# A two-layer hybrid encoder trunk on one core: expert places read into registers at the first load that needs them, another first buffer, and operands at other offsets

## The chip, the cores and the metric

The kernel runs on one core of one Trainium2 chip. The metric is the device time of one execution in microseconds, and less is better. The kernel before takes 1262.37 us, the median of three runs (1261.83 to 1262.54).

## What is computed

The reference is a trunk of two layers over 256 tokens of width 1024, in float32. Cut to what matters here:

```python
# layer 0
h = h + even_mixer(rmsnorm(h, g0), ...)   # retention heads and a causal convolution of 31 taps
h = h + swiglu(rmsnorm(h, g1), w_gate, w_up, w_down)      # inner width 2816
# layer 1
h = h + odd_mixer(rmsnorm(h, g2), ...)    # gMLP gating and a short convolution of 3 taps
h = h + moe_swiglu(rmsnorm(h, g3), router, e_gate, e_up, e_down)
                                          # 8 experts of inner width 3584, the best 2 for each token
return rmsnorm(h, final_norm)
```

All weights of all eight experts are read in any case: 3 x 1024 x 3584 x 4 bytes for each, 352 MB together, out of some 424 MB that the kernel moves.

## The kernel before

**Dense stages.** The products of layer 0 and of the mixer of layer 1 are made in three parts: each weight unit (1 MB, [128, 2048] float32) is split into a high part `hi` (ScalarE, L169) and a low part `lo` (VectorE, L172), the activations likewise, and `three_products` (L199, L202) sums high x high, low x high and high x low on TensorE. The activations are the weight-loaded operand, and `hi` or `lo` is streamed. Input projections take `xh` and `xl` (class `Norm`) in groups of 12 matmuls over four blocks of 128 rows. The products over rows take `sh`, `sl` (the convolved half of the output projection of layer 0, four blocks), `fh`, `fl` (`rows_product`, the down projection of 22 blocks) and `oyh`, `oyl` (`out_group`, the output projection of layer 1, eight blocks), in groups of six over two blocks, for two halves of the tokens and two of the columns.

**Offsets.** A tile pool gives each tile a fixed place in each partition of SBUF. By the program's allocation `raw`, `hi` and `lo` begin 32 bytes past a multiple of 512, `xh` and `xl` 288 past; in the pools "even" and "ffn" nearly every large tile, `sh`, `sl`, `fh` and `fl` among them, begins 96 past; in the pool "late" the tiles taken after `opc` (`swT`, `y0` with `oyh`, `y1` with `oyl`, `x1`, `x2`) begin 448 past.

**Experts.** The experts are handled in an order of places: place 0 is always expert 0, the others are the experts 1 to 7 by their number of tokens, most first. Which expert stands at a place is known only after routing: `places()` (L1128 on) counts the tokens on TensorE and VectorE, and ends in `idx_i` (L1153), an integer for each place. Each place has room for 96 or 64 tokens (`CAPS`) and is worked in the order `ORDER`, in two parts of 2048 and 1536 hidden columns. A part is 8 gate units and 8 up units (1 MB, or 768 KB in the second part), then 8 or 6 down units of 1 MB of the part before. TensorE works on units straight from the buffer into which they were loaded (`project_step` L1285, `down_step` L1303).

**The loads.** All weights stand in one list, `units`, and all loads are issued on SP's queue, in the order of that list (`Weights._load`, L135). An expert's unit has a callable as its source (`of_expert`), which is called when the load is emitted: for place 0 the address is fixed, for other places it takes `regs[place]`. Expert unit number i goes to `homes[i % 19]`: seven buffers `raw`, then `x1` (`raw_x1`, which held the padded input `spad` of the short convolution), `xl`, four times `hi` and `lo`, `y0` and `y1`. The first 17 are emitted while the output projection of layer 1 still runs, and afterwards `unit` emits, before the products of unit i, the loads up to i + 18. A load waits on SP until its buffer is free, and whatever SP was given after it waits too.

**Where the registers come from.** `places` runs behind unit 1 (the list `later`), and in it seven calls of `values_load` (L1155) read `idx_i` into registers of SP, one after another:

```python
for place in range(1, NE):
    regs[place] = nc.values_load(idx_i[0:1, place:place + 1], engines=(mybir.EngineType.SP,),
                                 min_val=0, max_val=NE - 1)
```

In SP's order they come after load 19 (emitted ahead of unit 1) and before load 20 (emitted ahead of unit 2). The first load that uses a register is number 40, the first gate unit of the second place, emitted ahead of unit 22.

Of the kernel before, what the change touches and what calls it, by code (L numbers as in the profile page):

```python
# [9 lines left out]
F32 = mybir.dt.float32  # L10
# [3 lines left out]
AF = mybir.ActivationFunctionType  # L14
# [4 lines left out]
P = 128  # L19
T = 256  # L20
TB = 2
D = 1024
# [5 lines left out]
CB = CH // P  # L28
# [4 lines left out]
NE = 8  # L33
# [3 lines left out]
N_RAW = 7  # L37
# [61 lines left out]
PE_TAPS = 9  # L99
TAP_CUTS = (6, 4, 16, 13, 13, 11, 10)  # L100
SCR = {"even": 7, "ffn": 5, "late": 6}


def f32(ap):
# [101 lines left out]
def overflow(nc, pool, wpool, small, w_gate, w_up, w_down, e, rank, wgt, slot, hn, h, ident,  # L206
# [5 lines left out]
    nc.vector.tensor_copy(wg, wgt[:, :, ds(e, 1)])  # L212
    oh = pool.tile([P, TB, P], F32, name="oh2", tag="scr", bufs=SCR["late"])
    for tb in range(TB):
# [61 lines left out]
def trunk_kernel(  # L276
# [9 lines left out]
    nc = tc.nc  # L286
# [44 lines left out]
    regs = {}  # L331

    def of_expert(w, place, view):

        def src():
            return view(w[0] if place == 0 else w[ds(regs[place], 1)].rearrange("o k n -> (o k) n"))
        return src

# [22 lines left out]
    wpool = ctx.enter_context(tc.tile_pool(name="weights", bufs=1))  # L361
# [6 lines left out]
    def ps_t():  # L368
        return psum.tile([P, CW], F32, name="pt", tag="pt", bufs=2)
# [5 lines left out]
    h = consts.tile([P, TB, D], F32, name="h")  # L375
# [15 lines left out]
    def load_gain(g, to):  # L391
        nc.sync.dma_start(to, g[0].rearrange("(k p) -> k p", p=P))
# [31 lines left out]
    def scr(pool, name):  # L424
        return pool.tile([P, CW], F32, name=name, tag="scr", bufs=SCR[pool.name])

# [16 lines left out]
    class Norm:  # L443
# [22 lines left out]
                low()  # L466

        def stats(self, tb):
            sq_ = self.pool.tile([P, D], F32, name="sqscr", tag="hid1" if self.pool.name == "late" else "big")
            nc.scalar.activation(sq_, h[:, tb, :], AF.Square, accum_out=self.ss[:, tb:tb + 1])  # L470

        def finish(self):
            rsqrt(self.rstd, self.ss, 1.0 / D)
# [51 lines left out]
    with tc.tile_pool(name="even", bufs=1) as pool, tc.manual_schedule():  # L525
        W.load_to(LOAD_A)
        for i, g in enumerate((e_norm_ffn, o_norm_mix, o_norm_ffn)):
            load_gain(g, gains[1][i * KB:(i + 1) * KB, :])
        prm = pool.tile([P, 2, P], F32, name="prm")
        nc.sync.dma_start(prm[:TAPS * CB, 0, :], e_dw_w[0].rearrange("j (b c) -> (j b) c", c=P))  # L530
        for i, v in enumerate((e_dw_b, e_cv_ln_g, e_cv_ln_b, e_ret_gn)):
            nc.sync.dma_start(prm[i * CB:(i + 1) * CB, 1, :], v[0].rearrange("(b c) -> b c", c=P))
# [75 lines left out]
        pc = pool.tile([P, 2, P], F32, name="pc")  # L608
# [260 lines left out]
    with tc.tile_pool(name="late", bufs=1) as pool:  # L869
# [6 lines left out]
        prm = scr(pool, "oprm")[:, :P]  # L876
# [17 lines left out]
        nc.sync.dma_start(lnb, row(o_sg_ln_b[0], CH))  # L894
        sgw = blocks(scr(pool, "sgw"))
        nc.sync.dma_start(sgw, o_sg_w[0].rearrange("g p q -> p g q"))
        pc = pool.tile([P, CB * 4], F32, name="opc")
        t = ps_t()
        nc.tensor.transpose(t[:, :CB * 4], prm[:CB * 4, :], ident[:CB * 4, :CB * 4])
        nc.vector.tensor_copy(pc, t[:, :CB * 4])  # L900
# [8 lines left out]
        x1 = pool.tile([P, 2 * D], F32, name="spad", tag="x1")  # L909
# [105 lines left out]
        def rt(name, n=NE):  # L1015
            return small.tile([P, TB, n], F32, name=name)
# [10 lines left out]
        with tc.manual_schedule():  # L1027
# [12 lines left out]
            for u in range(KB // 2 - 2):  # L1040
                w = W.next()
                for tb in range(TB):
                    for half in range(2):
# [5 lines left out]
            n = KB * max(CAPS)  # L1049
            rooms = {"xe": [r2[:, i * n:(i + 1) * n].rearrange("p (k n) -> p k n", k=KB) for i in range(2)],  # L1050
                     "oh": r2[:, 2 * n:2 * n + TB * P].rearrange("p (t n) -> p t n", t=TB)}

            homes = ([lambda: wpool.tile([P, 2 * D], F32, name="raw", tag="raw", bufs=N_RAW)] * N_RAW +
                     [lambda: pool.tile([P, 2 * D], F32, name="raw_x1", tag="x1")] +
                     [lambda: consts.tile([P, 2 * D], F32, name="raw_xl", tag="xl")] +
                     [lambda tag=tag: wpool.tile([P, 2 * D], F32, name="raw_" + tag, tag=tag, bufs=4)
                      for _ in range(4) for tag in ("hi", "lo")] +
# [63 lines left out]
        def by_place(dst, src, sel):  # L1121

            for tb in range(src.shape[1]):
                t = pool.tile([P, NE, NE], F32, name="picks", tag="picks", bufs=2)
                nc.vector.tensor_tensor(t, sel, src[:, tb:tb + 1, :].to_broadcast([P, NE, NE]), OP.mult)
                nc.vector.tensor_reduce(dst[:, tb, :], t, axis=AX.X, op=OP.add)

        def places():  # L1128

            pn = ps_t()  # L1130
            nc.tensor.matmul(pn[:, :NE], tri[:, 1, :], both[:, 0, :], start=True, stop=False)
            nc.tensor.matmul(pn[:, :NE], tri[:, 1, :], both[:, 1, :], start=False, stop=True)
            cnt = pool.tile([P, 1, NE], F32, name="cnt")
            nc.vector.tensor_copy(cnt[:, 0, :], pn[:, :NE])
            key = pool.tile([P, NE], F32, name="key")
            nc.vector.tensor_copy(key, cnt[:, 0, :])
            nc.vector.tensor_scalar(key[:, 0:1], key[:, 0:1], 2.0 * T, None, op0=OP.add)
            less = pool.tile([P, NE, NE], F32, name="less")
            nc.vector.tensor_tensor(less, key[:, None, :].to_broadcast([P, NE, NE]),
                                    key[:, :, None].to_broadcast([P, NE, NE]), OP.subtract)  # L1140
            nc.vector.tensor_tensor(less, less, thr[:, 0], OP.is_ge)
            at = pool.tile([P, 1, NE], F32, name="at")
            nc.vector.tensor_reduce(at[:, 0, :], less, axis=AX.X, op=OP.add)
            one = pool.tile([P, 1, NE], F32, name="one")
            nc.vector.tensor_scalar(one, at, 1.0, None, op0=OP.add)
            sel = pool.tile([P, NE, NE], F32, name="sel")
            nc.vector.tensor_tensor(sel, one.to_broadcast([P, NE, NE]),
                                    slot[:, :NE, None].to_broadcast([P, NE, NE]), OP.is_equal)
            idx = pool.tile([P, 1, NE], F32, name="idx")
            by_place(idx, slot[:, None, :NE], sel)  # L1150
            nc.vector.tensor_scalar(idx, idx, -1.0, None, op0=OP.add)
            idx_i = pool.tile([P, NE], I32, name="idx_i")
            nc.vector.tensor_copy(idx_i, idx[:, 0, :])  # L1153
            for place in range(1, NE):
                regs[place] = nc.values_load(idx_i[0:1, place:place + 1], engines=(mybir.EngineType.SP,),  # L1155
                                             min_val=0, max_val=NE - 1)
            ranks = rt("ranks")
            by_place(ranks, rank, sel)

            capacity = pool.tile([P, 1, NE], F32, name="capacity")  # L1160
            nc.vector.tensor_scalar(capacity, at, float(CAPS.index(64, 1)), None, op0=OP.is_ge)
            nc.vector.tensor_scalar(one, at, 0.0, None, op0=OP.is_equal)
            nc.vector.tensor_tensor(capacity, capacity, one, OP.add)
            nc.vector.tensor_scalar(capacity, capacity, -float(96 - 64), 96.0, op0=OP.mult, op1=OP.add)
            nc.vector.tensor_tensor(cnt, cnt, capacity, OP.subtract)
            most = pool.tile([P, 1], F32, name="most")
            nc.vector.tensor_reduce(most, cnt[:, 0, :], axis=AX.X, op=OP.max)
            nc.vector.tensor_scalar(most, most, 0.0, None, op0=OP.max)
            most_i = pool.tile([P, 1], I32, name="most_i")
            nc.vector.tensor_copy(most_i, most)  # L1170
            beyond = rt("beyond")
            for tb in range(TB):
                nc.vector.tensor_tensor(beyond[:, tb, :], rank[:, tb, :], capacity[:, 0, :], OP.subtract)
            gate_of.update(sel=sel, ranks=ranks, beyond=beyond, most_i=most_i)
# [25 lines left out]
        with tc.manual_schedule():  # L1200
# [31 lines left out]
            def results(place, acc, half):  # L1232

                yh = pool.tile([P, CW], F32R, name="eyh", tag="scr", bufs=SCR["late"])
                yl = pool.tile([P, CW], F32R, name="eyl", tag="scr", bufs=SCR["late"])
                n = CAPS[place]
# [115 lines left out]
            todo_[0]()  # L1352
            todo_[1]()
            later += [todo_[2], places, gates]
            acc = was = None
            for i, (place, p) in enumerate(steps):
# [126 lines left out]
```

## Time and profile before

| | |
|---|---|
| runs | 1262.54, 1262.37, 1261.83 us; median 1262.37 |
| the profiled execution | 1261.62 us, its span 1259.7 us |
| granted TensorE clock | 0.995 |
| busy in the span | PE 1213.3 us (96%), PEld 727.1, DVE 355.6, ACT 267.6 |
| DMA | 425.45 MB, mean 338 GB/s |

The span runs from the first to the last instruction; the profiled execution's own time is 1.9 us longer. PE is TensorE's matmuls, PEld its weight loads, DVE VectorE, ACT ScalarE; SPq is the sequencer of SyncE, which issues the DMAs. PE's busy time counts matmuls as they are pipelined, so a high share does not by itself make it the bound. A matmul's own duration overlaps the next one's; how fast matmuls follow each other is read from the times at which they start. The share of DMA is the mean busy share of 16 DMA engines.

### The profile page before, as it was taken

To read this page: it belongs to the slowest core of one execution; us is meant where nothing else is said; L and a number is where in the kernel's file an instruction comes from. 1 tells how busy PE (TensorE), PEld (TensorE's weight loads), DVE (VectorE), ACT (ScalarE), POOL (GpSimd) and SP (SyncE) were. 2 spreads that over 40 slices of the span, in tenths; PEclk is the share of its full clock that TensorE was granted. 3 is DMA by queue.
4 is the path that set the end of the run, shared out by engine and by line. 5 is a ranking of instruction groups with operands and counts; after the bars stand their busy time and mean duration, and the time that the engine had idled before them with its cause. 6 is when DMAs were issued, how large, how long until landed. Compare 5 with 4: busy or idle time off the path is not lost.

```text
span 1259.7 us, 26036 instructions
## 1 busy us (share of the span) xinstructions
PE 1213.3 (96%) x11611; PEld 727.1 (58%) x11611; DVE 355.6 (28%) x528; ACT 267.6 (21%) x358; POOL 0.2 (0%) x4
## 2 busy tenths in 40 slices
PE   8999999999999999999999999999999999997874
PEld 6886888888888443366457654336645764522211
DVE  6988655544773300010011001002000100100102
ACT  6547544433642200010000001001000100100001
POOL 0000000000000000000000000000000000000000
PEclk9999999999999999999999999999999999999997
DMA  8923555556648799999999999999999999999993
GB/s 285 350 72 123 212 201 171 176 187 200 214 168 330 299 417 419 417 415 418 418 415 417 418 415 416 419 419 415 419 417 405 416 419 410 412 419 419 407 413 127
DMA packets 90598, 425.45 MB, mean 338 GB/s; under 512 B 8500, under 2 KB 15984, under 8 KB 61168
## 3 DMA queue, kind: packets, MB, share of 16 engines
q1 hardware_dynamic: 90480, 423.72, 85.0%
q8 instruction: 93, 1.52, 0.5%
q14 instruction: 25, 0.20, 0.0%
HBM read 422.64 MB, written 1.05 MB: 336 GB/s over the span
## 4 chain that ended last, share of the span: by engine, by line
PE 82%; DMA 14%; DVE 1%; ACT 1%; issue 0%; SPq 0%; ACTq 0%; DVEq 0%
PE gu L1285 33%; PE gu L199 18%; PE acc L1303 15%; PE gu L202 9%; DMA raw<-in_o_exp_up_dram 4%; DMA raw_lo<-in_o_exp_down_dram 3%; DMA raw<-in_o_exp_down_dram 3%; DMA raw_hi<-in_o_exp_down_dram 2%; DMA raw_y<-in_o_exp_gate_dram 2%; PE pt L436 1%; PE pt L1322 1%; PE pt L1210 1%; DMA raw_lo<-in_o_exp_gate_dram 1%; PE acc L652 1%; PE gu L776 1%; PE pt L1258 1%
## 5 line engine op out<-in xcount | busy, mean ns | idle before, releaser
L1285 PE MATMUL gu<-raw,rooms 128*32 128x512 f32 (+2 forms) x2070 | 190.1, 512 | 5.9 <-DMA raw<-in_o_exp_up_dram 4.6
L1370 DVE TENSOR_TENSOR esg<-gu,esg 128x512 f32<-128x512 f32 (+2 forms) x40 | 24.2, 623 | 524.8 <-PE gu L1285 524.8
L172 DVE TENSOR_TENSOR lo<-raw,hi 128x2048 fp32r<-128x2048 f32 (+1 forms) x63 | 139.8, 2222 | 90.6 <-ACT hi L169 90.6
L1285 PEld LDWEIGHTS gu<-raw,rooms 128*32 128x32 f32 x2070 | 86.6, 110 | 101.8 <-issue 70.7
L199 PE MATMUL gu<-hi,xh 128*128 128x512 f32 (+1 forms) x368 | 141.2, 387 | 0.9 <-ACT hi L169 0.6
L199 PE MATMUL gu<-hi,xl 128*128 128x512 f32 (+1 forms) x368 | 139.9, 383 | 0.2 <-DVE xl L462 0.2
L169 ACT CAST hi<-raw 128x2048 fp32r<-128x2048 f32 (+1 forms) x63 | 116.4, 1859 | 86.8 <-PE gu L199 85.7
L1285 PE MATMUL gu<-raw_lo,rooms 128*32 128x512 f32 (+2 forms) x1142 | 113.2, 515 | 2.1 <-DMA raw_lo<-in_o_exp_gate_dram 1.1
L1285 PE MATMUL gu<-raw_hi,rooms 128*32 128x512 f32 (+2 forms) x1142 | 112.9, 515 | 1.4 <-DMA raw_hi<-in_o_exp_up_dram 0.8
L1303 PE MATMUL acc<-raw,hx 128*32 128x512 f32 (+1 forms) x1044 | 95.9, 510 | 3.1 <-DMA raw<-in_o_exp_down_dram 3.0
L202 PE MATMUL gu<-lo,xh 128*128 128x512 f32 (+1 forms) x368 | 95.7, 381 | 0.1
L1285 PEld LDWEIGHTS gu<-raw_lo,rooms 128*32 128x32 f32 x1142 | 47.3, 110 | 58.3 <-issue 44.6
L1285 PEld LDWEIGHTS gu<-raw_hi,rooms 128*32 128x32 f32 x1142 | 47.7, 110 | 57.0 <-issue 43.4
L1329 ACT COPY hx<-pt 128x512 f32<-128x512 f32 x24 | 14.1, 586 | 310.6 <-PE pt L1322 310.6
L199 PEld LDWEIGHTS gu<-hi,xh 128*128 128x128 f32 x368 | 69.2, 188 | 13.9 <-ACT hi L169 0.9
L1366 ACT ACTIVATE esg<-gu 128x512 f32<-128x512 f32 (+2 forms) x40 | 20.9, 543 | 263.9 <-PE gu L1285 263.9
L199 PEld LDWEIGHTS gu<-hi,xl 128*128 128x128 f32 x368 | 69.3, 188 | 13.1 <-DVE xl L462 0.5
L202 PEld LDWEIGHTS gu<-lo,xh 128*128 128x128 f32 x368 | 67.0, 188 | 13.6 <-DVE lo L172 0.5
L1303 PEld LDWEIGHTS acc<-raw,hx 128*32 128x32 f32 x1044 | 42.0, 110 | 49.7 <-issue 25.8
L1303 PE MATMUL acc<-raw_lo,hx 128*32 128x256 f32 (+1 forms) x648 | 56.8, 483 | 3.0 <-DMA raw_lo<-in_o_exp_down_dram 3.0
L1303 PE MATMUL acc<-raw_hi,hx 128*32 128x512 f32 (+1 forms) x628 | 55.7, 488 | 1.8 <-DMA raw_hi<-in_o_exp_down_dram 1.8
L1285 PE MATMUL gu<-raw_y,rooms 128*32 128x512 f32 (+2 forms) x570 | 54.0, 509 | 1.2 <-DMA raw_y<-in_o_exp_gate_dram 1.1
(287 smaller groups left out, 1063.4 us busy)
## 6 DMA issues: line engine op xcount, KB each, us to landing
raw<-in_o_exp_down_dram SPq DMA_DIRECT2D x41, 1024.0 KB
raw<-in_o_exp_gate_dram SPq DMA_DIRECT2D x27, 1024.0 KB
raw_hi<-in_o_exp_down_dram SPq DMA_DIRECT2D x23, 1024.0 KB
raw_lo<-in_o_exp_down_dram SPq DMA_DIRECT2D x23, 1024.0 KB
raw<-in_o_exp_up_dram SPq DMA_DIRECT2D x21, 1024.0 KB
raw<-in_o_exp_gate_dram SPq DMA_DIRECT2D x25, 768.0 KB
raw<-in_o_exp_up_dram SPq DMA_DIRECT2D x23, 768.0 KB
raw_hi<-in_o_exp_up_dram SPq DMA_DIRECT2D x15, 1024.0 KB
```

What stands on the lines that cost most here:

```text
L169: self.nc.scalar.copy(hi[:, k, :], raw[:, k, :])
L172: self.nc.vector.tensor_tensor(lo[:, k, :], raw[:, k, :], f32(hi[:, k, :]), OP.subtract)
L199: nc.tensor.matmul(ps, x(a), wh(b), start=(first and n == 0), stop=(last and n == total - 1))
L202: nc.tensor.matmul(ps, xh(a), wl(b), start=False, stop=(last and n == total - 1))
L436: nc.tensor.transpose(t[:, j * P:(j + 1) * P], src[:, j * P:(j + 1) * P], ident)
L652: nc.tensor.matmul(pcv[b // 2][:, (b % 2) * T:(b % 2 + 1) * T], dgs[j], tap_in(b, j)[0], start=(j == 0), stop=(j == PE_TAPS - 1))
L776: nc.tensor.matmul(pss[tb][half], yr[:, k, tok(tb)], wo[k // 2][:, k % 2, c], start=(k == 0), stop=False)
L1285: nc.tensor.matmul(ps[a][q * STRIP:(q + 1) * STRIP, o0:o0 + n], xe[:, k, g * STRIP:(g + 1) * STRIP], raw[:, 0, c0:c0 + n], start=(k == 0 a ...
L1303: nc.tensor.matmul(acc[bank][q * STRIP:(q + 1) * STRIP, o0:o0 + n], hT[:, a * CW + o:a * CW + o + STRIP], raw[:, k, c0:c0 + n], start=(p[0 ...
L1329: nc.scalar.copy(hT[:, a * CW:a * CW + n], t[:, :n])
L1366: nc.scalar.activation(sg[:, :n], ps[:, :n], AF.Silu)
L1370: nc.vector.tensor_tensor(sg[:, :n], ps[:, :n], sg[:, :n], OP.mult)
```

## The change

The register reads leave `places` and are made, one for each place, in the source of the first load that needs the place. `x1` becomes the first of the 19 homes. Three tiles are padded, `sqscr` in the pool "ffn" and `prm` in "even" by 48 floats (192 bytes) and `opc` in "late" by 24 floats (96 bytes), so that the tiles of these pools taken after them move by as much.

```diff
+SHIFT = {"even": 48, "ffn": 48, "late": 24}
...
         def src():
+            if place and place not in regs:
+                regs[place] = nc.values_load(regs["of"][0:1, place:place + 1], engines=(mybir.EngineType.SP,),
+                                             min_val=0, max_val=NE - 1)
             return view(w[0] if place == 0 else w[ds(regs[place], 1)].rearrange("o k n -> (o k) n"))
...
         def stats(self, tb):
-            sq_ = self.pool.tile([P, D], F32, name="sqscr", tag="hid1" if self.pool.name == "late" else "big")
-            nc.scalar.activation(sq_, h[:, tb, :], AF.Square, accum_out=self.ss[:, tb:tb + 1])
+            n = D + (SHIFT["ffn"] if self.pool.name == "ffn" else 0)
+            sq_ = self.pool.tile([P, n], F32, name="sqscr", tag="hid1" if self.pool.name == "late" else "big")
+            nc.scalar.activation(sq_[:, :D], h[:, tb, :], AF.Square, accum_out=self.ss[:, tb:tb + 1])
...
-        prm = pool.tile([P, 2, P], F32, name="prm")
+        prm = pool.tile([P, 2 * P + SHIFT["even"]], F32, name="prm")[:, :2 * P].rearrange("p (a n) -> p a n", a=2)
...
-        pc = pool.tile([P, CB * 4], F32, name="opc")
+        pc = pool.tile([P, CB * 4 + SHIFT["late"]], F32, name="opc")[:, :CB * 4]
...
-            homes = ([lambda: wpool.tile([P, 2 * D], F32, name="raw", tag="raw", bufs=N_RAW)] * N_RAW +
-                     [lambda: pool.tile([P, 2 * D], F32, name="raw_x1", tag="x1")] +
+            homes = ([lambda: pool.tile([P, 2 * D], F32, name="raw_x1", tag="x1")] +
+                     [lambda: wpool.tile([P, 2 * D], F32, name="raw", tag="raw", bufs=N_RAW)] * N_RAW +
...
-            for place in range(1, NE):
-                regs[place] = nc.values_load(idx_i[0:1, place:place + 1], engines=(mybir.EngineType.SP,),
-                                             min_val=0, max_val=NE - 1)
+            regs["of"] = idx_i
```

## Rows read from the trace of the kernel before

**Rows 1.** Busy time by stretch: PE, PEld, DVE, ACT, POOL, clock, DMA share, GB/s

```profile
252.00:325.00 73.00, 73.00 (x359) 60.38 (x358) 34.05 (x26) 26.60 (x19) 0.00 (x0) 1.00 0.54 181
...
440.00:540.00 100.00, 98.84 (x1072) 35.58 (x1068) 7.24 (x13) 5.86 (x11) 0.00 (x0) 1.00 1.01 418
...
1140.00:1236.00 96.00, 77.45 (x702) 21.39 (x694) 8.40 (x13) 5.93 (x10) 0.00 (x0) 1.00 0.99 402
```

**Rows 2.** Timeline of PE late in the experts: start, us, what, idle before

```profile
1129.01 1.92 PE L1285 MATMUL gu<-raw_hi,rooms 128*32 128x512 f32 x16 [0.58 <-DMA raw_hi<-in_o_exp_gate_dram]
1131.50 1.92 PE L1285 MATMUL gu<-raw_lo,rooms 128*32 128x512 f32 x16 [0.57 <-DMA raw_lo<-in_o_exp_gate_dram]
```

**Rows 3.** Busy time by stretch, as in rows 1, around the register reads

```profile
420.00:433.00 13.00, 13.00 (x123) 3.87 (x126) 6.87 (x43) 4.24 (x6) 0.00 (x0) 1.00 0.43 132
423.00:430.00 7.00, 7.00 (x68) 2.08 (x64) 5.91 (x39) 1.49 (x2) 0.00 (x0) 1.00 0.11 42
...
430.00:431.00 1.00, 1.00 (x16) 0.30 (x12) 0.14 (x1) 0.00 (x0) 0.00 (x0) 1.00 0.77 104
```

**Rows 4.** Timeline of SP: loads of the first expert as they are issued

```profile
353.02 35.12 SPq L135 DMA_DIRECT2D raw<-in_o_exp_gate_dram  x7
388.20 0.42 SPq L135 DMA_DIRECT2D raw_x<-in_o_exp_gate_dram  x1
...
404.89 0.33 SPq L135 DMA_DIRECT2D raw_hi<-in_o_exp_up_dram  x1
...
409.09 1.07 SPq L135 DMA_DIRECT2D raw_y<-in_o_exp_gate_dram  x2
419.69 11.88 SPq L135 DMA_DIRECT2D raw<-in_o_exp_gate_dram  x5
```

**Rows 5.** SP's wait for idx_i (total, times, longest), and the reads of line 1155

```profile
SPq L1155 <- DVE idx_i L1153: 4.8, 1, 4.8
...
L1155 SPq TENSOR_LOAD <-idx_i x7: 262/266/465, 424.9 to 428.9; - x7
```

**Rows 6.** Timeline of PE over the first expert's units

```profile
419.93 1.92 PE L1285 MATMUL gu<-raw,rooms 128*32 128x512 f32 x16
...
421.93 8.79 PE L1285 MATMUL gu<-raw,rooms 128*32 128x512 f32 x80
430.53 1.90 PE L1285 MATMUL gu<-raw_x,rooms 128*32 128x512 f32 x16
432.25 1.90 PE L1285 MATMUL gu<-raw_xl,rooms 128*32 128x512 f32 x16
```

**Rows 7.** SP's waits over the whole span: total, times, longest

```profile
SPq L135 <- DMA raw<-in_o_exp_gate_dram: 70.2, 41, 3.5
```

**Rows 8.** Timeline of SP: load 40 and the four after it

```profile
459.83 9.21 SPq L135 DMA_DIRECT2D raw<-in_o_exp_gate_dram  x5
```

**Rows 9.** Timeline of VectorE: the last readers of the short convolution's input

```profile
364.88 1.67 DVE L949 SCALAR_TENSOR_TENSOR vn<-spad,opc,vn 128x256 f32<-128x256 f32 x4
```

**Rows 10.** Timeline of PE: starts of matmuls with xh, with fh, and with oyh

```profile
141.23 0.39 PE L199 MATMUL gu<-hi,xh 128*128 128x512 f32 x1
...
146.67 0.39 PE L199 MATMUL gu<-hi,xh 128*128 128x512 f32 x1
...
269.99 0.39 PE L199 MATMUL gu<-hi,fh 128*128 128x512 f32 x1
...
271.39 0.39 PE L199 MATMUL gu<-hi,fh 128*128 128x512 f32 x1
...
389.32 0.40 PE L199 MATMUL gu<-hi,oyh 128*128 128x512 f32 x1
...
390.72 0.40 PE L199 MATMUL gu<-hi,oyh 128*128 128x512 f32 x1
```

**Rows 11.** Groups of matmuls up to 410 us, by shape: count, busy us, mean ns

```profile
L199 PE MATMUL gu<-hi,fh 128*128 128x512 f32 x88 | 35.0, 397 | 0.0
...
L199 PE MATMUL gu<-hi,oyh 128*128 128x512 f32 x32 | 13.0, 407 | 0.0
```

## The prediction, made before the changed kernel ran

> **What bounds the kernel now.** I read first how the load on the DMA queue divides by stage. From 440 us to the end of the loads it runs full, 418 GB/s at a share of 1.01 and still 402 GB/s between 1140 and 1236 us, while the dense stages use about half of it (0.54 between 252 and 325 us, with PE busy for all 73 us) [rows 1]. So there are two bounds: TensorE up to about 416 us, the queue after that. The second can be seen at TensorE: late in the experts every unit of 16 matmuls begins with 0.57 us of waiting for a load, and units begin 2.49 us apart although one takes 1.92 us [rows 2]. A load of 1 MB at 418 GB/s is 1.0486 / 0.418 = 2.5 us, the same number. What the queue loses after 416 us is therefore lost for good, and there is one such place: from 420 to 433 us its share is 0.43, from 423 to 430 us 0.11 [rows 3]. That is 13 x 0.57 = 7.4 us without work.
>
> The cause is in SP's order. I number the experts' loads from 0. Loads 17 and 18 go to y0 and y1 at 409.09 us; load 19, first of the five to raw at 419.69 us, needs the buffer of unit 0 and goes out as that is done; the five end at 419.69 + 11.88 = 431.57 us [rows 4]. Between load 19 and load 20 stand the register reads of L1155: SP waited 4.8 us for idx_i, and seven reads then began between 424.9 and 428.9 us, 0.67 us apart, so that the last ended at about 429.5 us [rows 5]. Yet the next buffers came free early: unit 1 starts at 419.93 us, and 80 records from 421.93 us are units 2 to 6 at 1.72 us each [rows 6]. Load 20 could have gone at 421.9 us. No load before number 40, the first of place 1, uses a register.
>
> **The change, part by part.**
>
> *Reads moved.* The seven reads (each a register load, a register operation and an assertion) and their one wait leave the place after load 19; one read now stands ahead of the first load of each later place, from load 40 on. Removed is the hole. Loads 20 to 25 go out as units 1 to 6 end (the first at 421.9 us, then about every 1.72 us) instead of at 429.5 us and later; each is 768 KB, 0.786 / 0.418 = 1.88 us of the queue, so buffers now come free faster than the queue moves and it stays full. Not all 7.4 us come back: from 420 to 423 us the queue already waited for load 19, which the change leaves where it is. That part is 7.4 less the 7 x 0.89 = 6.2 us of 423 to 430 us [rows 3], less what is lost while the queue starts again (0.77 of 430 to 431 us is busy, with only 104 GB/s); I put 0.6 us to load 19 and take 6.8 us, with 6.0 and 7.4 as ends.
>
> Added is 0.67 us of SP ahead of loads 40, 86 and so on, (428.9 - 424.9) / 6 per read [rows 5]. In the full stage SP waits for the queue before nearly every load, 70.2 us in 41 waits on one group of them [rows 7], so 1.7 us cover 0.67. If that cover were gone, loads in flight would cover it. Queued behind each read are only later loads on SP; the wait for idx_i is over by 424.8 us.
>
> *Does the lead survive?* Buffers could become the limit, as after the hole SP has no more of them than units set free. Between the hole and load 40, issued at 459.83 us [rows 8], 12 loads of 0.786 MB and 8 of 1.049 MB went out, 17.8 MB; from about 430.5 us on [rows 3] the queue moved 29.3 x 0.418 = 12.2 MB. So 5.6 MB, 13 us of transfer, were in flight when buffers were scarcest. With the queue 6.8 us ahead 6 us remain in flight, and it does not run dry. At the end TensorE already waits for each load and needs 1.92 us per 2.49 us: it makes up 6.8 us within some ten units.
>
> *x1 first.* Load 0 goes to the buffer of the short convolution. SP then waits for its last reader, which ends at 364.88 + 1.67 = 366.55 us [rows 9], where before it issued to raw at 353.02 us. Behind it stand loads 1 to 3, 13.5, 7 and 4 us late. Unit 1 takes its load at 419.93 us and unit 2 at 421.93 us [rows 6], so nobody waits. One load more is through before 388.20 us, when raw_x went out; but the next ones wait for the hi and lo buffers until 404.89 us [rows 4], so the queue only idles sooner. I take nothing; bounds: no loss, since load 19 stays tied to unit 0, and 0.6 us of gain if load 19 finds the queue empty.
>
> *Offsets.* PE's weights (hi, lo) start 32 bytes past a multiple of 512; xh and xl, which it multiplies with in the input projections, 288 past; fh, fl, sh, sl 96 past; oyh, oyl 448 past. The padding moves the latter to 288, 288 and 32: all alike modulo 256. In a projection 24 matmuls take 146.67 - 141.23 = 5.44 us, 226.7 ns each; with fh and fl six take 1.40 us, 233.3 ns, and with oyh and oyl also six in 1.40 us [rows 10]. 88 x 3 + 32 x 3 + 16 x 3 = 408 matmuls are of the slower kind [rows 11]; the last 48, with sh and sl, are counted from the loops and priced as fh. If the offset is what makes them slow, 408 x 6.67 ns = 2.7 us go, all in stages where PE is never idle; everything behind, the experts' first buffers too, comes that much sooner. Ends: nothing, and 2.7 us. The page "SBUF — State Buffer" of the Trainium skill, section on the two separate sides, says that TensorE's port never waits on anyone; by that the term would be nothing. The rows do not refute it, since the slow groups also work on two blocks at a time, the fast on four. I take 2.7 us: the same 233.3 ns appears at two different offsets, and no group away from 32 modulo 256 runs at 226.7. VectorE's and the experts' operands move too; I price that at nothing, as units from raw_x (448 now) and raw (32) start the same 1.72 us apart [rows 6].
>
> The sum: the profiled execution took 1261.62 us; less 6.8 and 2.7 is 1252.1. The median of the runs lies 0.75 above it: **1252.9 us**.
>
> **Rivals.** *The offsets do nothing*, the two-block order being the cause: 1262.37 - 6.8 = 1255.6 us. For it speaks that every slow group has that order; against, that an order by itself needs a reason to cost 6.67 ns at each matmul, inside groups as well as at their ends. The Trainium skill's page named above would come out at this time too. *The queue gives the gain back*: with the loads ahead, SP meets full buffers in the stages with 96-row experts, and only the offsets remain: 1262.37 - 2.7 = 1259.7 us. Against it stands the 13 us in flight.
>
> *Slower*: a register read on SP holds up the loads behind it until those in flight have landed. Before, the reads came when the queue was all but empty [rows 3, 5], so the trace hardly shows them beside traffic. Its place would be each first load of the seven later places; its price the restart seen after the hole, from the first issue at 429.5 us to a queue that is barely moving before 431 us, 1.5 us, with the read on top 2.2 us. Seven make 15 us: 1252.9 + 15 = 1268 us. It decides from 9.5 / 7 = 1.4 us per read. Against it: the first read, of at most 0.465 us at 424.9 us, ended while the queue still moved a little. *The change doing nothing* would need SP to have waited for buffers and not for idx_i, which [rows 5, 6] exclude.
>
> **How the numbers follow.** Both gains 0.66; no gain from offsets 0.23; gain of the queue given back 0.07; slower 0.04. The likeliest case alone spans 1251.4 to 1254.4 (6.0 to 8.0 us from the queue and x1, 2.0 to 2.7 us from the offsets, 0.3 us for the measurement). The second, with 6.0 to 7.4 us, reaches 1256.4. Range: 1251.4 to 1256.6. About 0.2% (2.5 us) is what a measurement of this kernel tells from no change. The first two cases are faster by more; the third lies at the border, 0.04 of it counted faster, 0.03 same. So 0.93, 0.03, 0.04.
>
> **What would show it.** After the change: a queue share near 1 where it was 0.11; loads 20 to 25 some 1.7 to 2 us apart; seven single reads spread over the experts, the queue full around each; six matmuls with fh and fl in 1.36 us instead of 1.40, and the first expert matmul about 2.7 us sooner; the last load some 9.5 us sooner. Wrong would be a hole that merely moves to a later load, dips of the queue at the reads, or waits for buffers that empty it.

## The result, and the profile after

The changed kernel takes 1274.28 us (median of four runs, 1273.41 to 1275.05) against 1262.30 us for the kernel before, run beside it. The ratio is 1.0099 with a 95% interval of 1.0087 to 1.0111: 12 us slower. I had forecast 1252.9 and a range up to 1256.6.

At first sight two of the three parts did what was forecast. First the queue by stretch, columns as in [rows 1, 3], changed kernel:

```profile
382.00:400.00 18.00, 18.00 (x85) 14.77 (x84) 6.67 (x8) 3.26 (x4) 0.00 (x0) 1.00 0.33 117
400.00:413.00 13.00, 12.91 (x88) 10.00 (x87) 8.47 (x18) 4.43 (x8) 0.00 (x0) 1.00 0.45 164
413.00:420.00 7.00, 6.78 (x172) 3.22 (x174) 1.38 (x7) 2.03 (x3) 0.00 (x0) 1.00 0.31 89
...
423.00:430.00 7.00, 7.00 (x72) 2.14 (x68) 4.04 (x28) 2.08 (x3) 0.00 (x0) 1.00 1.00 421
...
440.00:540.00 100.00, 94.99 (x1017) 34.74 (x1013) 7.24 (x13) 5.86 (x11) 0.00 (x0) 1.00 1.01 418
```

The hole of [rows 3] is closed: share 1.00 instead of 0.11 from 423 to 430 us (what closes it here, the moved reads or something else, is asked below). But ahead of it stands a new and larger one. The same three early stretches of the kernel before:

```profile
382.00:400.00 18.00, 18.00 (x83) 14.51 (x82) 6.99 (x6) 4.29 (x5) 0.00 (x0) 1.00 0.78 306
400.00:413.00 13.00, 13.00 (x81) 10.24 (x80) 7.65 (x13) 4.43 (x8) 0.00 (x0) 1.00 1.00 408
413.00:420.00 7.00, 6.69 (x171) 4.17 (x172) 2.76 (x10) 0.37 (x1) 0.00 (x0) 1.00 1.01 419
```

What emptied the queue stands in SP's timeline of the changed kernel, which answers to [rows 4]:

```profile
351.19 35.12 SPq L137 DMA_DIRECT2D raw<-in_o_exp_gate_dram  x7
406.28 0.80 SPq L137 DMA_DIRECT2D raw_y<-in_o_exp_gate_dram  x2
407.13 0.42 SPq L137 DMA_DIRECT2D raw_x<-in_o_exp_gate_dram  x1
417.38 0.33 SPq L137 DMA_DIRECT2D raw<-in_o_exp_gate_dram  x1
417.76 0.43 SPq L137 DMA_DIRECT2D raw_xl<-in_o_exp_up_dram  x1
...
426.25 0.33 SPq L137 DMA_DIRECT2D raw_lo<-in_o_exp_gate_dram  x1
428.79 7.81 SPq L137 DMA_DIRECT2D raw<-in_o_exp_gate_dram  x4
```

Read it against what I forecast. The first seven loads still go to raw, at about the old times (351.19 us for 353.02); none goes to x1. Between 386 and 406 us SP issues nothing, and then three loads from the second half of the gate (loads 17, 18 and 19, to y0, y1 and x1). The eighth gate unit, load 7, goes to a raw at 417.38 us, and loads 8 to 16 stand behind it until 426.25 us; before, they went out between 388 and 409 us. So SP no longer issues in the order of the list, as it did in the kernel before: loads 17 to 19 stand ahead of loads 7 to 16. What sets the order on SP no run tells. SP's waits between 380 and 420 us (total, times, longest), the two that bear on it:

```profile
SPq L137 <- PE gu L204: 17.7, 1, 17.7
SPq L137 <- PE pt L1227: 10.1, 1, 10.1
```

The first is for TensorE's products with oyh, which lies in y0, and ends when load 17 goes out; the second ends when load 7 goes out. With load 7 ahead of load 17 SP would have stood at load 7 for all of that time, to the same 417 us. The time 417.38 us is the end of unit 0, as TensorE's timeline of the changed kernel shows (unit 0 in its first line, unit 1 in its last):

```profile
415.42 1.91 PE L1289 MATMUL gu<-raw,rooms 128*32 128x512 f32 x16
417.26 0.44 PE L1227 MATMUL pt<-ident,rooms 128*128 128x128 f32 x2
417.62 1.92 PE L1289 MATMUL gu<-raw,rooms 128*32 128x512 f32 x16
```

So load 7 waits for the end of unit 0, that is for the buffer in which load 0 lies. The code says why, and I had misread it. `Weights.next` emits the loads up to nine ahead of the unit in use (`LOADS = 9`). At its last call before the list of homes is made, two dense units are still to be used, so 9 - 2 = 7 expert loads are out already, all to raw by the default of `_load`. The list serves only from load 7 on. With raw seven times at its head that made no difference; with x1 at its head, load 7 takes index 7, which is now a raw, and all seven raws are full.

The bill is paid in bytes. From 382 to 440 us (58 us) the queue moved 318 GB/s before, 18.4 MB, and 228 GB/s after, 13.2 MB. The missing 5.2 MB are 12.5 us of a queue that runs at 418 GB/s from there on [rows 1] (415 from 640 to 1140 us); the span grew by 1272.1 - 1259.7 = 12.4 us.

The offsets show in groups of six matmuls. Changed kernel, from one group's start to the next (1.36 us, against 1.40 in [rows 10]), first with fh, then with oyh:

```profile
269.59 0.39 PE L201 MATMUL gu<-hi,fh 128*128 128x512 f32 x1
...
270.95 0.39 PE L201 MATMUL gu<-hi,fh 128*128 128x512 f32 x1
...
387.44 0.39 PE L201 MATMUL gu<-hi,oyh 128*128 128x512 f32 x1
...
388.80 0.39 PE L201 MATMUL gu<-hi,oyh 128*128 128x512 f32 x1
```

The first expert matmul comes at 415.42 us instead of 417.73, 2.31 us sooner. The line of the kernel before:

```profile
417.73 1.91 PE L1285 MATMUL gu<-raw,rooms 128*32 128x512 f32 x16
```

The single reads are there too, seven of them over the experts, with no dip of the queue:

```profile
L339 SPq TENSOR_LOAD <-idx_i x7: 264/269/480, 468.8 to 1111.8; - x7
```

### The profile page after: what moved, and what is told of

Its sections match the earlier page's. It is cut to its first block, busy times and chain, and to the rows that moved or that the text cites. A ratio compares the mean times of both kernels' runs of the same rounds, so it can differ in the third digit from the quotient of the medians.

```text
span 1272.1 us, 26027 instructions
## 1 busy us (share of the span) xinstructions
PE 1215.4 (96%) x11611; PEld 728.9 (57%) x11611; DVE 355.6 (28%) x528; ACT 267.5 (21%) x358; POOL 0.2 (0%) x4
## 4 chain that ended last, share of the span: by engine, by line
PE 73%; DMA 24%; DVE 2%; ACT 1%; issue 0%; SPq 0%; ACTq 0%; DVEq 0%
PE gu L1289 27%; PE gu L201 17%; PE acc L1307 12%; PE gu L204 9%; DMA raw<-in_o_exp_down_dram 6%; DMA raw<-in_o_exp_up_dram 6%; DMA raw_hi<-in_o_exp_down_dram 3%; DMA raw_lo<-in_o_exp_down_dram 3%; DMA raw_y<-in_o_exp_gate_dram 2%; DMA raw<-in_o_exp_gate_dram 2%; DMA raw_lo<-in_o_exp_gate_dram 2%; DMA raw_hi<-in_o_exp_gate_dram 2%; PE pt L441 1%; PE pt L1214 1%; PE acc L658 1%; PE pt L1326 1%
```

## The experiments

Theory H is the one above (homes): load 7 waits for load 0's buffer. Rival R is the one that I had priced on the slow side (a register read holds the queue), rival O that the offsets of the experts' operands slow the experts. In the code below each home is written short, by its tag.

**One part undone: the old order of homes.** The change with its reads and offsets, and

```diff
-            homes = ([x1] + [raw] * N_RAW +
+            homes = ([raw] * N_RAW + [x1] +
```

> The change with the old order of homes (x1 eighth again), reads moved and offsets moved as in the change. Theory H (homes): the first seven expert loads are issued to raw before the list of homes is made, so the list is used from load 7 on; with x1 at its head, load 7 falls to raw, to the very buffer in which load 0 lies, and SP waits there for the end of unit 0 (417.4 us) with loads 8 to 16 behind it. With the old order this is gone, and the two other parts show their gains: 1262.3 less 6.8 (hole closed) less 2.3 to 2.7 (offsets; the first expert matmul came 2.31 us sooner in the changed kernel) is 1253 us (1251.5 to 1255); load 7 at about 386 us, share of the queue over 0.95 from 420 to 433 us. Rival R (reads): the seven single reads hold up the queue and cost the 12 us and the gain too: still about 1274. Rival O (offsets of the experts' operands slow the experts): still about 1274.

Measured: 1254.17 us, ratio to the kernel before 0.9943 (0.9930 to 0.9957). This beats both kernels. The queue in the stretch that lost the 5.2 MB:

```profile
382.00:440.00 58.00, 57.69 (x524) 34.52 (x526) 23.92 (x72) 12.76 (x19) 0.00 (x0) 1.00 0.94 370
```

And load 7 in SP's timeline of this run:

```profile
387.14 0.43 SPq L137 DMA_DIRECT2D raw_x<-in_o_exp_gate_dram  x1
```

Load 7 goes to x1 at 387.14 us, 30 us sooner than in the changed kernel, and the queue moves 370 GB/s instead of 228. From 423 to 430 us it does not reach what I expected: share 0.94 at 318 GB/s. R and O fall with this one run: reads and offsets are in it.

**One part alone: x1 first.** The kernel before with nothing but the two lines exchanged.

> The kernel before with x1 at the head of the homes and nothing else. Theory H: loads 7 to 16 go out from 417 to 428 us instead of 386 to 409, and the queue loses what the changed kernel lost, without the 2.3 us of the offsets: 1274.3 + 2.3 = 1276.6 us (1274 to 1279). The register reads now stand behind load 16 with eight loads in flight, so their hole costs nothing more. Rivals R and O: 1262.3, no change, since the reads and the offsets are the old ones.

Measured: 1276.37 us, 1.0122 (1.0106 to 1.0137); 212 GB/s from 382 to 440 us. H had 1276.6. Two exchanged lines make the whole loss and 2.7 us more. The hole at the reads, which are at their old place here, is filled by the held loads:

```profile
423.00:430.00 7.00, 7.00 (x69) 2.08 (x64) 5.91 (x39) 1.49 (x2) 0.00 (x0) 1.00 1.02 425
```

**One part alone: the reads.** The loop at the end of `places` gone, the read in `of_expert`.

> The kernel before with the reads moved to the first load of each place and nothing else. Theory H: the hole is closed and nothing given back: 1262.3 - 6.8 = 1255.5 us (1254.5 to 1256.5); share of the queue over 0.95 from 423 to 430 us. Rival R: each read holds the queue for some 3 us, seven of them 21 us, so 1255.5 + 21 = 1276 us, with dips of the queue at each read. Rival O: 1255.5.

Measured: 1256.25 us, 0.9959 (0.9945 to 0.9973): 5.5 us faster; the interval, 3.4 to 6.9 us, just holds the 6.8 forecast. The row for 423 to 430 us shows what is missing:

```profile
423.00:430.00 7.00, 7.00 (x68) 2.08 (x64) 5.91 (x38) 1.49 (x2) 0.00 (x0) 1.00 0.95 313
```

The share is 0.95, as I wrote, but the rate is 313 GB/s, three quarters of 418. SP's timeline of this run, with the load to y0 and y1 ahead of loads 19 to 23:

```profile
409.39 0.86 SPq L135 DMA_DIRECT2D raw_y<-in_o_exp_gate_dram  x2
420.06 7.98 SPq L135 DMA_DIRECT2D raw<-in_o_exp_gate_dram  x5
```

From 410.3 to 420.06 us SP issues nothing, as load 19 waits for unit 0, and the queue runs down. Then loads come singly, about 2 us apart. By the trace's semaphore events load 20 lands 3.8 us after load 19 and load 21 2.6 us after load 20; 1.9 us is the step from there on. So the wait of load 19, which the change leaves, costs more than the 0.6 us that I put to it: 318 GB/s became 358 from 382 to 440 us, which is worth 5.6 us.

**One part alone: the offsets.**

> The kernel before with the three paddings and nothing else. Theory H and rival R: 408 matmuls at 226.7 ns instead of 233.3, 2.7 us sooner at most; the first expert matmul 2.3 us sooner as in the changed kernel; the queue's hole starts sooner by as much: 1262.3 - 2.3 = 1260 us (1259.5 to 1260.5). Rival O: slower than 1262.3, up to 1281 if it is to explain the whole loss.

Measured: 1259.91 us, 0.9987 (0.9978 to 0.9996): 1.8 us faster (0.5 to 2.8). O is out.

**x1 really first.** The change as it is, with one line more where the convolution's buffer is made, so that load 0 takes its home from the list too:

```diff
         x2 = pool.tile([P, 2 * D], F32, name="vn", tag="x2")
+        W.place[first_unit] = lambda: pool.tile([P, 2 * D], F32, name="raw_x1", tag="x1")
```

> The change as it is, but load 0 too takes its home from the list, so that it really goes to x1, and load 7 to the seventh raw, which is free. Theory H (the loss is load 7 waiting for the buffer in which load 0 lies): the loss is gone, 1254 us (1253 to 1255.5) as with the old order; load 0 is issued at about 365 us instead of 351 and nobody waits for it. Rival X (x1 at the head is itself what costs, SP waiting there for the last reader of the convolution's input, with all loads behind it late): still 1274, or between.

Measured: 1254.03 us, 0.9937 (0.9923 to 0.9951), the same as with the old order. Load 0 now goes out fourth, at 365.27 us, 14 us later than in the changed kernel, with three loads to raw ahead of it and four behind it, and nobody misses it. SP's timeline:

```profile
351.66 9.68 SPq L137 DMA_DIRECT2D raw<-in_o_exp_gate_dram  x3
365.27 0.33 SPq L137 DMA_DIRECT2D raw_x<-in_o_exp_gate_dram  x1
369.98 16.79 SPq L137 DMA_DIRECT2D raw<-in_o_exp_gate_dram  x4
386.86 0.38 SPq L137 DMA_DIRECT2D raw_xl<-in_o_exp_up_dram  x1
```

The price of nothing that I put on this wait was right, but it was the price of something that the change doesn't do. Nor does the wait come about as I drew it: loads 1 to 3 do not stand behind load 0, they go out first, from 351.66 us on.

**x1 seventh.** It leaves the head of the list, but index 7 stays a raw:

```diff
-            homes = ([x1] + [raw] * N_RAW +
+            homes = ([raw] * (N_RAW - 1) + [x1] + [raw] +
```

> The change with x1 as the seventh home, index 6, and the seventh raw behind it, index 7. Theory H: load 7 takes home 7, a raw, as in the changed kernel, and waits for unit 0: 1274 us (1273 to 1276), loads 7 to 16 issued from 417 us. Rival X: x1 isn't at the head any more, so 1254.

Measured: 1276.17 us, 1.0114 (1.0099 to 1.0130). Rival X is out: the place of x1 is of no account, that of the raws is. It is 14.4 us slower than the kernel before, the changed kernel 12.0; of the 2.4 us between them 1.9 can be put to one load of 768 KB, since there load 19 went to x1 at 407.13 us and here it has to wait for a raw. SP's timeline of this run:

```profile
351.16 35.13 SPq L137 DMA_DIRECT2D raw<-in_o_exp_gate_dram  x7
406.27 0.80 SPq L137 DMA_DIRECT2D raw_y<-in_o_exp_gate_dram  x2
417.37 0.33 SPq L137 DMA_DIRECT2D raw<-in_o_exp_gate_dram  x1
```

**Half the dose: the occupied raw at index 12.** Loads 7 to 11 find free homes (`raw_`, `lo_` and so on are the homes by their tags):

```diff
+            homes = [raw_] * 6 + [lo_, x1_, xl_, hi_, lo_, hi_, raw_, lo_, hi_, lo_, hi_, y0_, y1_]
```

> The change with the list turned so that loads 7 to 11 find free homes (x1, xl, hi, lo, hi) and the one raw that is still taken comes at index 12: five loads (12 to 16) are held up instead of ten. Theory H: the loss follows the bytes held. Ten loads of 10.2 MB, 24.5 us of queue, cost 19.7 us against the old order, so 4.8 us of them were not lost; five loads are 4.98 MB, 11.9 us, less 4.8 gives 7 us, in proportion 9.8: 1261 to 1264 us, with loads 12 to 16 issued from 417 us. If it is a stall of fixed length on SP, whatever stands behind it: 1274.

Measured: 1263.91 us, 1.0016 (1.0007 to 1.0026), 9.7 us above the old order, at the proportional end of what was expected. The loss goes with the bytes held up; the wait itself ends at nearly the same time as in the changed kernel, as SP's timeline of this run shows (the held load in the second line):

```profile
406.64 0.81 SPq L137 DMA_DIRECT2D raw_y<-in_o_exp_gate_dram  x2
417.74 0.33 SPq L137 DMA_DIRECT2D raw<-in_o_exp_up_dram  x1
```

**Each read eight times.** On the kernel with the old order:

```diff
-                regs[place] = nc.values_load(...)
+                for _ in range(8):
+                    regs[place] = nc.values_load(...)
```

> The reads and the offsets of the change, the old order of homes, and each of the seven reads made eight times over: 5.4 us on SP ahead of each place's first load instead of 0.67. If reads are covered by the loads in flight, as I priced them (13 us in flight when buffers were scarcest, 6 after the gain; up to eight loads, 20 us, later): 1254.2 us, at most 1 us more, at the first of the seven. If each read holds the queue, 7 reads more at each of 7 places at 0.67 us are 33 us: up to 1287.

Measured: 1253.96 us, 0.9942 (0.9926 to 0.9957). 56 reads cost nothing. The first eight begin at 456.3 us (the row of their line: count, shortest, median and longest ns, first and last start):

```profile
L340 SPq TENSOR_LOAD <-idx_i x56: 262/263/470, 456.3 to 1094.7; - x56
```

Load 40, behind them, goes out at 461.33 us, and the queue does not notice:

```profile
450.00:460.00 10.00, 9.21 (x162) 4.51 (x158) 0.56 (x1) 1.06 (x3) 0.00 (x0) 1.00 1.01 414
460.00:470.00 10.00, 10.00 (x132) 4.09 (x128) 0.29 (x1) 0.19 (x1) 0.00 (x0) 1.00 1.01 418
```

**Other offsets**, on the kernel with the old order, `SHIFT` alone changed: first 16, 40 and 32 floats, then 32, 8 and 56.

> The old order of homes and the moved reads, with other paddings: sh and sl start at 160 modulo 256 and 512, fh and fl at 0 modulo 256 (256 modulo 512), oyh and oyl at 64. The streamed hi and lo stay at 32. Theory A (a matmul is 6.67 ns slower unless the weight-loaded operand starts as the streamed one does, modulo 256): all three slow, a mean step of 233.3 ns where the change has 227, six fh matmuls in 1.40 us, and the time 2 us above the 1254.2 with the offsets of the change, 1256. Theory B (alike modulo 128 is enough): sh at 227, fh and oyh at 233.3. Theory C (the weight-loaded operand's own start matters, not its relation to the streamed one: 96 and 192 are bad, the others not): all three at 227 and 1254.

> As the run before, with sh and sl at 224 modulo 256, fh and fl at 128, oyh and oyl at 160. Theory A: all three at 233.3 ns, 1256 us. Theory B: oyh at 227, sh and fh at 233.3. Theory C: nothing excluded; with all starts measured, the bad ones can be listed.

Measured: 1256.84 and 1254.55 us, one run each, too few for 2 us. The traces say more. Mean step between starts of neighbouring matmuls (those under 260 ns), by the start of the weight-loaded operand modulo 256, with the number of steps:

```
xh xl    32: 227 to 228 (all kernels)
sh sl    96: 233.4 (44)   160: 231.9 (44)   224: 229.2 (44)   32: 227.7 (44)
fh fl    96: 233.3 (256)    0: 233.3 (256)  128: 234.2 (256)  32: 227.0 (256)
oyh oyl 192: 233.2 (88)    64: 233.4 (88)   160: 233.2 (88)   32: 228.0 (88)
```

In the first of the two, with oyh at 64, six matmuls take 1.40 us again:

```profile
388.09 0.40 PE L201 MATMUL gu<-hi,oyh 128*128 128x512 f32 x1
...
389.49 0.40 PE L201 MATMUL gu<-hi,oyh 128*128 128x512 f32 x1
```

32 is the fastest start for every operand, 224 lies between, the other six are slow. B and C are out. A holds but for 224, which it had at 233.3. Whether 32 is good in itself or because hi and lo start there stays open: hi and lo were never moved. The paddings also move the other tiles of the same pools; no run moves an operand alone.

**All kernels on one line of reasoning.** If the queue is the bound from 440 us on, a kernel's time against the kernel before is the difference of the bytes moved until then, at 418 GB/s:

| kernel | GB/s, 382 to 440 us | worked out, us | measured, us |
|---|---|---|---|
| before | 318 | 0 | 0 |
| changed | 228 | +12.5 | +12.0 |
| old order | 370 | -7.2 | -7.5 |
| x1 first alone | 212 | +14.7 | +14.7 |
| reads alone | 358 | -5.6 | -5.5 |
| offsets alone | 334 | -2.2 | -1.8 |
| x1 seventh | 215 | +14.3 | +14.4 |
| raw at 12 | 303 | +2.1 | +2.1 |
| reads eightfold | 375 | -7.9 | -7.9 |
| x1 really first | 355 | -5.1 | -7.8 |
| other offsets, first | 359 | -5.7 | -5.5 (one run) |
| other offsets, second | 361 | -6.0 | -7.8 (one run) |

Worked out: (318 - rate) x 58 us / 418, with the rates of one profiled execution each. Eight kernels besides the one before agree to 0.5 us. The kernel with x1 really first agrees as well, once what it moved earlier is counted. By 382 us the others had all moved at 197 GB/s on average and this one at 200, which is another 2.7 us. The kernel before and this one:

```profile
0.00:382.00 382.00, 377.21 (x1770) 305.76 (x1771) 249.71 (x311) 196.24 (x226) 0.20 (x4) 1.00 0.58 197
0.00:382.00 382.00, 377.38 (x1776) 307.68 (x1777) 250.43 (x312) 196.96 (x226) 0.20 (x4) 1.00 0.59 200
```

Of the two single runs the second is 1.8 us off; single runs of one kernel here lie up to 3.6 us apart (raw at 12: 1262.01 to 1265.56). The table tells where the time was lost, not why: the why rests on the edits.

## Why the prediction was wrong, step by step

**The bound**: right. The differences, the second single run apart, are settled by what the queue has moved when it becomes full.

**Reads moved**: right in kind, mis-sized. The term was -6.8 us with ends 6.0 and 7.4; alone it measured -5.5 (-3.4 to -6.9), and by the queue's bytes -5.6. The sentence that failed is "buffers now come free faster than the queue moves and it stays full": it stays busy at 313 GB/s, since it had run down during load 19's wait. By that the 0.6 us that I put to load 19 should have been about 0.6 + 6.8 - 5.5 = 1.9.

**The lead**: right. The queue is full around load 40 even with 5 us of reads ahead of it. The reads' own price of nothing is right as well.

**x1 first**: this step failed, at its first words, "Load 0 goes to the buffer of the short convolution". It does not: the first seven loads never see the list. Load 7 goes to a raw that is still full, and loads 8 to 16 wait behind it until 417 us. Priced at nothing with bounds of no loss and 0.6 us of gain, the step costs 14.7 us alone. My bounds covered the size of a wait and left out that the buffers might be dealt out otherwise. The trace of before could not show it, as list and default agree for seven loads; the nine-ahead rule of `next` and the point at which the list is made do. The two other steps by themselves give the kernel with the old order, 1254.17 us, inside the range given for the whole.

**Offsets**: right in kind, near in size: -2.7 forecast, -1.8 measured (-0.5 to -2.8). The first expert matmul came 2.31 us sooner in the changed kernel and 1.53 with the old order (416.20 us). I had weighed it against the page "SBUF — State Buffer" of the Trainium skill, by whose section on the two separate sides TensorE's port never waits on anyone, which I read as a term of nothing. The same instructions on the same data went from 233.3 to 227.0 ns as the tiles of their pools moved, so the term is not nothing. Whether TensorE waits for its port or loses the time elsewhere no run tells, so the section's sentence itself is neither borne out nor refuted.

**The rivals.** The slower one, with 0.04, named the reads. The time did come out on the slow side, 6 us beyond that rival's 1268, but by a buffer and not by a read. *The offsets do nothing* is out: the groups over two blocks kept their order and still went to 227.0 ns. *The queue gives the gain back* did not happen: with the old order it moves 415 GB/s from 640 to 1140 us, before 416. But SP does wait more for buffers that TensorE holds, 98.1 us in 95 waits of one kind where it was 28.5 in 42 (SP's waits with the old order: total, times, longest):

```profile
SPq L137 <- PE gu L1289: 98.1, 95, 2.7
```

Why the whole change is 12.0 us slower and not 14.7 - 5.5 - 1.8 = 7.4: the held loads themselves fill the hole at 423 us, so the moved reads had next to nothing left to give.

## What to carry to other kernels

Where buffers are dealt out from a rotating list, find the first load that really takes its buffer from it, and follow the list by hand until it meets a buffer that is still full. Here the one load that needed such a buffer held nine behind it, though their homes came free between 387 and 407 us, as the run with the old order shows. Read from the trace which loads stand behind it: three that come later in the list had been put ahead. When one queue is the bound of a long last stage, count the bytes it has moved when that stage begins: that number gave the time of nine kernels to 0.5 us, all but the two of one run each.

## What was not expected of the hardware

A DMA share of 0.95 can go with three quarters of the rate: 313 GB/s where the queue had run down and loads of 768 KB were sent singly, against 418 at 1.01 with many in flight. And where the weight-loaded operand starts, or what else moves with it in its pool, is worth 4 to 7 ns of the 227 between two matmuls of 512 columns: with a start at 32 modulo 256 they are fast, at 0, 64, 96, 128, 160 and 192 slow where these were tried, and 224 costs 1.5 ns (229.2 against 227.7).
